# Two FFN pairs' last products put in a row on TensorE, in a hybrid decoder layer on one Trainium2 core

## The chip, the cores and the metric

The kernel runs on one core of one Trainium2 chip. The metric is the device time of one execution in microseconds, as the median over runs. Engines are named as in the profile: PE is TensorE's matmul, PEld its weight load, DVE is VectorE, ACT ScalarE, POOL GpSimd, SP SyncE, which here issues nearly all DMAs.

## What is computed

One layer of a decoder trunk: a token mixer (mLSTM beside attention over a memory), then a squared-ReLU MLP, each behind an RMSNorm and with a residual sum, and a last RMSNorm. The change lies in the first matrix product of the MLP.

```
D_MODEL = 1024; SEQ = 1024; D_FF = 4 * D_MODEL          # all float32
def squared_relu_mlp(h, w1, w2):
    return jnp.square(jax.nn.relu(h @ w1)) @ w2
x = x + mlstm_mixer(rms_norm(x, norm_mix0), mem_k, mem_v, ...)
x = x + squared_relu_mlp(rms_norm(x, norm_ffn0), w_ff1_0, w_ff2_0)
return rms_norm(x, final_norm)
```

## The kernel before

**Number format.** Every float32 operand of a matmul is split into a high and a low part of the type fp32r: the high part is a copy by ScalarE (L88, L91, L806), the low part the difference between source and high part (L103, L771, L809), on VectorE or GpSimd. `mm3` (L108) then makes three matmuls, high times high (L110), high times low (L111), and low times high (L112). So the first matmul of a product waits for the left operand's high part, the third for its low part.

**The MLP's first product.** The hidden features come in 16 pairs of two 128-row blocks, the tokens in two halves of 512. Each pair is a 2 x 2 block product, computed with seven products instead of eight (the Strassen-Winograd scheme). Products have the names "1" to "7". Product i is `product1` (L871): four blocks of the contraction by `mm3`, twelve matmuls of 128 x 512 into one PSUM bank. Their left operands come from the weights: 1, 2 and 4 are the blocks 11, 12 and 22 themselves; 5, 6, 7 and 3 are the sums S1, S2, S3 and S4. `w_parts` (L694) loads the raw blocks, makes the sums (L722), and `make` (L751) splits them. The sums lie in three buffers (tag "sum"), the raw blocks in rings of their own, the split operands in five buffers (tag "w"). The right operands (B11, B21, B22, T1 to T4) are made once from the two halves of the normed input; T3 and T4 lie in the tile xa, and the parts of T4 and B22 are made last, by `other_half` (L799), which is a generator: `go_on(n)` (L1022) takes n of its steps.

**One pair's result.** Bank X collects products 1, 6, 7 and 4 one after the other, and is copied out in between; Y holds product 2, and Z 5 and 3. The sums are

- `first_part` (L938), `second_part` (L962), `third_part` (L969), `product5` (L977), `product7` (L981): products 1, 2, 6, 5, 7 with the copies out of X
- `sixth_part` (L985): h22 = copy + Z (L991), squared ReLU, writes of the planes 0 and 6
- `fourth_part` (L998): product 4, h21 by squared ReLU out of X, write of plane 1
- `fifth_part` (L1004): product 3, h12 = copy + Z (L1007), squared ReLU (L879, L880), four sums for the second matrix product (L1011 to L1014), and one write of four planes, 1 MB (L1015)

A pair's results go into a tile hq of seven planes (tag "qk", two buffers in all), and from there to HBM (hd). Pairs 0 to 5 have had products 1 and 2 beforehand, in `early` (L885), while the second half's input was normed. In all texts here 4_0 means product 4 of pair 0.

**The order.** The loop over ROW (L1026) runs the pairs 0, 1, 6, 2, 7, 3, ... and writes the products out by hand, pair by pair; matmuls of `product1` and some VectorE operations keep that order (`tc.keep_in_program_order`). All others are placed by a scheduler, which takes the code's order as its starting point and each engine's list is then run strictly in order. On TensorE the products around the change stand as 6_0, 5_0, 7_0, 6_1, 5_1, 7_1, 4_0, 1_6, 3_0, 4_1, 2_6, 3_1, 6_6, 5_6, 7_6, 6_2, 4_6. For pair 0 and pair 1 the low parts are VectorE's (`lows`, `on`). `first_part_of` (L84) puts each high part behind the one before it on ScalarE, through `queue`.

Of the kernel before, what the change touches and what calls it, by code (L numbers as in the profile page):

```python
# [8 lines left out]
F32 = mybir.dt.float32  # L9
F32R = mybir.dt.float32r  # L10
AF = mybir.ActivationFunctionType
# [3 lines left out]
P = 128  # L15
# [3 lines left out]
HT = 512  # L19
# [16 lines left out]
def trunk_kernel(ctx, tc, a, out):  # L36
    nc = tc.nc
    V, A, G, T = nc.vector, nc.scalar, nc.gpsimd, nc.tensor
# [3 lines left out]
    qkx = ctx.enter_context(tc.tile_pool(name="qkx", bufs=2))  # L42
# [4 lines left out]
    def ps(name):  # L47
        return psum.tile([P, 512], F32, tag="ps", name=name)
# [33 lines left out]
    queue = []  # L82
# [609 lines left out]
    ROW = [0, 1, 6, 2, 7, 3, 8, 4, 9, 5, *range(10, NPAIR)]  # L692

    def w_parts(pool, srcs, nm, homes=None, on=None, both=None, on_v="36"):  # L694
# [51 lines left out]
            for key in keys:  # L746
                load(key)

        get.again = again

        def make(i, lows):  # L751
            if i == "1":
# [125 lines left out]
    def relu_square(dst, src):  # L878
        A.activation(dst, src, AF.Relu)  # L879
        A.activation(dst, dst, AF.Square)  # L880
# [57 lines left out]
    def first_part(p):  # L938
        o = begun.get(p) or Pair()
        o.w = pair_parts(p, on=V if p == 1 else None) if p else a0  # L940
        if p not in begun:
            o.p, o.X, o.Y, o.Z = p, ps(f"fX{p}"), None, None
            product1(o.X, o.w("1"), "1", True)
        if p == 0:
            o.s = [None, hraw[0][:, 1], hraw[1][:, 0]]
        elif p == 1:
            o.s = [None, hraw[1][:, 1], cm.tile([P, HT], F32, tag="rms_r", name="hs_1")]
        elif p == ROW[2]:
            o.s = [hraw[0][:, 0], None, None]
        else:  # L950
            home(o)
        if p in begun:
            o.s[0] = o.s0
        else:
            A.activation(o.s[0], o.X, AF.Copy)
        return o

    def home(o):
        o.h = qkx.tile([P, 7, HT], F32, tag="qk", name=f"hq{o.p}")
        o.s = [o.h[:, SLOT[i]] for i in "173"]  # L960

    def second_part(o):  # L962
# [14 lines left out]
    def product5(o):  # L977
        o.Z = ps(f"fZ{o.p}")
        product1(o.Z, o.w("5"), "5", True)

    def product7(o):  # L981
        product1(o.X, o.w("7"), "7", False)
        A.activation(o.s[2], o.X, AF.Copy)  # L983

    def sixth_part(o):  # L985
        if o.p < 2:
            o.h = qkx.tile([P, 7, HT], F32, tag="qk", name=f"hq{o.p}")
        else:
            product7(o)
        h22 = o.h[:, SLOT["3"]]  # L990
        V.tensor_tensor(h22, o.s[2], o.Z, ALU.add)  # L991
        if o.p in begun:
            relu_square(o.h[:, SLOT["1"]], o.s[0])
        relu_square(h22, h22)
        for n in (0, 6):
            nc.sync.dma_start(hd[o.p, :, n], o.h[:, n])

    def fourth_part(o):  # L998
        product1(o.X, o.w("4"), "4", False)
        h21 = o.h[:, SLOT["2"]]  # L1000
        relu_square(h21, o.X)
        nc.sync.dma_start(hd[o.p, :, 1], o.h[:, 1])

    def fifth_part(o):  # L1004
        product1(o.Z, o.w("3"), "3", False)
        h12 = o.h[:, SLOT["7"]]
        st["h12"] = V.tensor_tensor(h12, o.s[1], o.Z, ALU.add).ins  # L1007
        relu_square(h12, h12)
        if o.p < NPAIR - 2:
            h11, h21, t2, t1, _, t4, h22 = (o.h[:, n] for n in range(7))  # L1010
            V.tensor_tensor(t1, h12, h11, ALU.subtract)  # L1011
            V.tensor_tensor(h12, h22, h12, ALU.subtract)
            V.tensor_tensor(t2, h22, t1, ALU.subtract)
            V.tensor_tensor(t4, h21, t2, ALU.subtract)  # L1014
            nc.sync.dma_start(hd[o.p, :, 2:6], o.h[:, 2:6])  # L1015
        else:
            nc.sync.dma_start(hd[o.p, :, 4], o.h[:, 4])

    begun, steps, sum_up = early()
    begun, old = {o.p: o for o in begun}, None  # L1020

    def go_on(n):  # L1022
        for _ in range(n):
            next(steps, None)

    for p in ROW:  # L1026
        cur = first_part(p)
        if p == 0:
            cur.w.again("12", "22")
            third_part(cur)  # L1030
            sum_up(begun[BEGUN - 1])
            go_on(4)
            product5(cur)
            go_on(2)
            product7(cur)
        elif p == 1:
            third_part(cur)
            go_on(1)
            product5(cur)
            go_on(3)  # L1040
            product7(cur)
            go_on(4)
            sixth_part(old)
            fourth_part(old)
            first = old
        elif p in begun:
            third_part(cur)
            fourth_part(old)
            fifth_part(old)
            product5(cur)  # L1050
            sixth_part(cur)
        else:
            if p == ROW[2]:
                go_on(4)
                sixth_part(old)
                fifth_part(first)
            fourth_part(old)
            second_part(cur)
            fifth_part(old)
            third_part(cur)  # L1060
            product5(cur)
            sixth_part(cur)
        old = cur
# [69 lines left out]
    last_pair, old = old, None  # L1133
    queue.clear()
    for c in range(NCH - 1):
        rights = {}
        for q in range(2):
# [3 lines left out]
            cur = quarter_first(c, q, rights)  # L1141
# [19 lines left out]
            old = cur  # L1161
# [134 lines left out]
```

## Time and profile before

| | us |
|---|---|
| runs: lowest, median, highest of 3 | 1080.66, 1084.4, 1086.15 |
| the profiled execution | 1080.86 |
| its span, first to last instruction | 1079.1 |
| busy in the span: PE, PEld | 1041.6, 888.9 |
| busy in the span: DVE, POOL, ACT | 704.8, 601.2, 547.4 |

The mean granted TensorE clock is 0.985 of full speed. Times in the rows count from the span's start. In a timeline a row is one instruction, or several alike ones merged (x2); its columns are start, duration, engine, line, operation, output and inputs, and in brackets how long the engine was idle before it and who released it. Buffer numbers are left out, so that w_a is any left operand of the MLP's first product and S_a any sum.

### The profile page before, as it was taken

Reading aid. Unit: us, or ns where it says so; the run is one execution under the profiler, and the core shown is the slowest. Engines: PE = TensorE matmul, PEld = TensorE weight load, DVE = VectorE, ACT = ScalarE, POOL = GpSimd, SP = SyncE. Lnnn points to the kernel's source line nnn. Section 1 sums busy time; section 2 is a strip of 40 time slices with the busy share of each in tenths; the row PEclk is TensorE's granted clock in tenths of the full one; section 3 lists DMA queues with packets and bytes.
Section 4 is the critical chain, followed back from the end, with each engine's and each line's share of the span. In section 5 each row is a group of like instructions: output and inputs, shape, how many; then the busy total and the mean of one; then the engine's idle time right before and its main releaser. Section 6 shows DMA issues by size and latency. Waiting matters only on the chain.

```text
span 1079.1 us, 14619 instructions
## 1 busy us (share of the span) xinstructions
PE 1041.6 (97%) x5014; PEld 888.9 (82%) x5014; DVE 704.8 (65%) x1139; ACT 547.4 (51%) x1062; POOL 601.2 (56%) x457
## 2 busy tenths in 40 slices
PE   9989999999999999987999999999999999999995
PEld 7988898899998888865888888887878888888894
DVE  6586885952767467983544343443889888878567
ACT  6376664344754454563555555555355334443273
POOL 6546434554434474012755656555678777786446
PEclk9998999999999999998999999999999999999997
DMA  7444342233323566214654544346756555544224
GB/s 214 106 132 132 91 127 80 67 99 89 91 67 107 161 192 195 78 58 162 200 181 170 195 166 157 127 156 233 252 189 196 152 160 163 150 136 136 60 70 155
DMA packets 81802, 152.46 MB, mean 141 GB/s; under 512 B 8096, under 2 KB 27584, under 8 KB 79936
## 3 DMA queue, kind: packets, MB, share of 16 engines
q1 hardware_dynamic: 81584, 151.51, 44.7%
q8 instruction: 39, 0.64, 0.2%
q14 instruction: 35, 0.29, 0.1%
q10 hardware_dynamic: 144, 0.03, 0.0%
HBM read 114.52 MB, written 36.19 MB: 140 GB/s over the span
## 4 chain that ended last, share of the span: by engine, by line
PE 77%; DVE 9%; DMA 6%; ACT 3%; issue 2%; POOL 2%; SPq 0%; DVEq 0%; POOLq 0%; ACTq 0%
PE fX L112 5%; PE fX L110 5%; PE fX L111 5%; PE gX L110 4%; PE gX L111 4%; PE gX L112 4%; DMA hr<-hd 4%; PE wo L110 3%; PE wo L112 3%; PE wo L111 3%; PE fZ L110 2%; PE fZ L112 2%; PE fZ L111 2%; PE gZ L111 2%; PE gZ L112 2%
## 5 line engine op out<-in xcount | busy, mean ns | idle before, releaser
L116 DVE TENSOR_TENSOR hb<-hr,hb 128x1024 fp32r<-128x1024 f32 x53 | 87.6, 1653 | 10.6 <-ACT hb L115 10.3
L1094 DVE TENSOR_TENSOR xo<-xo,gX 128x512 f32<-128x512 f32 x112 | 74.5, 682 | 26.1 <-PE gX L112 22.8
L111 PE MATMUL gX<-hb,w_b 128*128 128x512 f32 x224 | 87.3, 390 | 0.5 <-DVE hb L116 0.5
L110 PE MATMUL gX<-hb,w_b 128*128 128x512 f32 x224 | 86.2, 391 | 0.6 <-DVE xo L1094 0.6
L112 PE MATMUL gX<-hb,w_b 128*128 128x512 f32 x224 | 85.2, 390 | 0.8 <-POOL w_b L771 0.8
L91 ACT ACTIVATE w_b<-S_b 128x512 fp32r<-128x512 f32 x56 | 34.8, 629 | 75.9 <-PE gX L112 31.8
L771 POOL TENSOR_TENSOR w_b<-r_b,w_b 128x512 fp32r<-128x512 f32 x42 | 68.2, 1636 | 8.6 <-ACT w_b L91 8.6
L103 POOL TENSOR_TENSOR w_wo<-r_wo,w_wo 128x512 fp32r<-128x512 f32 x32 | 45.3, 1423 | 49.1 <-ACT w_wo L91 47.7
L115 ACT ACTIVATE hb<-hr 128x1024 fp32r<-128x1024 f32 x53 | 55.8, 1053 | 33.1 <-DMA hr<-hd 32.8
L771 POOL TENSOR_TENSOR w_a<-r_a,w_a 128x512 fp32r<-128x512 f32 x30 | 39.8, 1327 | 52.8 <-ACT w_a L88 52.0
L722 POOL TENSOR_TENSOR S_b<-r_b,r_b 128x512 f32<-128x512 f32 x28 | 46.5, 1661 | 28.8 <-DVE w_b L771 24.7
L103 POOL TENSOR_TENSOR w_o<-r_o,w_o 128x384 fp32r<-128x384 f32 x32 | 34.4, 1081 | 47.1 <-ACT w_o L91 47.1
L112 PE MATMUL fX<-xa,w_a 128*128 128x512 f32 x128 | 51.7, 404 | 7.7 <-DVE w_a L771 7.7
L103 POOL TENSOR_TENSOR w_v<-r_v,w_v 128x388 fp32r<-128x388 f32 x32 | 40.0, 1261 | 33.4 <-ACT w_v L91 33.3
L103 POOL TENSOR_TENSOR w_qk<-r_qk,w_qk 128x384 fp32r<-128x384 f32 x32 | 38.5, 1219 | 25.9 <-ACT w_qk L91 25.8
L88 ACT ACTIVATE w_a<-S_a 128x512 fp32r<-128x512 f32 x63 | 39.1, 625 | 24.8 <-PE fZ L112 14.5
L110 PE MATMUL fX<-xa,w_a 128*128 128x512 f32 x128 | 51.1, 399 | 0.2 <-ACT hq L983 0.2
L111 PE MATMUL fX<-xa,w_a 128*128 128x512 f32 x128 | 51.2, 400 | 0.0
L110 PE MATMUL wo<-xa,w_wo 128*128 128x512 f32 x128 | 51.0, 399 | 0.0
L110 PEld LDWEIGHTS gX<-hb,w_b 128*128 128x128 f32 x224 | 42.1, 188 | 10.3 <-DVE xo L1094 1.7
L112 PEld LDWEIGHTS gX<-hb,w_b 128*128 128x128 f32 x224 | 42.0, 188 | 10.0 <-POOL w_b L771 1.2
L111 PE MATMUL wo<-xa,w_wo 128*128 128x512 f32 x128 | 50.1, 391 | 0.0
(392 smaller groups left out, 3471.6 us busy)
## 6 DMA issues: line engine op xcount, KB each, us to landing
hr<-hd SPq DMA_DIRECT2D x53, 512.0 KB, 3.7
hd<-hq SPq DMA_DIRECT2D x14, 1024.0 KB, 4.1
r_b<-w_ff SPq DMA_DIRECT2D x56, 256.0 KB, 2.9
hd<-hq SPq DMA_DIRECT2D x50, 256.0 KB, 2.0
r_a<-w_ff SPq DMA_DIRECT2D x36, 256.0 KB, 2.7
r_wo<-w_out SPq DMA_DIRECT2D x32, 256.0 KB, 2.7
r_a<-w_ff SPq DMA_DIRECT2D x13, 512.0 KB, 4.5
r_v<-w_v SPq DMA_DIRECT2D x32, 194.0 KB, 2.4
```

What stands on the lines that cost most here:

```text
L88: i = A.activation(dst, src, AF.Copy)
L91: A.activation(dst, src, AF.Copy)
L103: i = engine.tensor_tensor(w[:, 1, :n], raw[:, :n], w[:, 0, :n], ALU.subtract)
L110: keep(T.matmul(out, lhsT=lh, rhs=rh, start=start, stop=False, skip_group_check=goes_on))
L111: keep(T.matmul(out, lhsT=lh, rhs=rl, start=False, stop=False, skip_group_check=goes_on))
L112: keep(T.matmul(out, lhsT=ll, rhs=rh, start=False, stop=stop, skip_group_check=goes_on))
L115: A.activation(hi, src, AF.Copy)
L116: V.tensor_tensor(lo, src, hi, ALU.subtract)
L722: i = (on or G).tensor_tensor(t, x, y, op)
L771: low = engine.tensor_tensor(w[:, 1], src, w[:, 0], ALU.subtract)
L1094: V.tensor_tensor(x, x, banks[e], ALU.add)
```

## The change

Nothing is added to or taken from the work; it is put in another order.

- `get.add_up` becomes callable from the loop, and `result(o)` allocates a pair's tile hq on its own.
- In pair 0's turn, pair 1's first part is begun before product 7 of pair 0: its sums S1 and S2 and the left operand of 6_1 are made there. ScalarE's copy of 7_0 out of the bank is placed behind that left operand's high part.
- In pair 1's turn, the left operand of 4_0 is made right behind the code of 5_1. 4_0 then comes before pair 0's sum h22, no longer behind it.
- At the head of pair 6's turn (ROW[2]) stand 4_1, the left operands of 3_0 and 3_1, then 3_0 with pair 0's last sums, and pair 1's h22. Only then comes pair 6's own first part.

On TensorE the products then stand as 6_1, 5_1, 7_1, 4_0, 4_1, 3_0, 1_6, 2_6, 3_1, 6_6, 5_6, 7_6, 6_2, 4_6. Lines behind L983 have other numbers in the new kernel: L991 becomes L994, L1007 L1010, L1011 to L1014 L1014 to L1017, L1015 L1018.

```diff
-        get.again = again
+        get.again, get.add_up = again, add_up
...
+    def result(o):
+        o.h = qkx.tile([P, 7, HT], F32, tag="qk", name=f"hq{o.p}")
+
     def home(o):
-        o.h = qkx.tile([P, 7, HT], F32, tag="qk", name=f"hq{o.p}")
+        result(o)
         o.s = [o.h[:, SLOT[i]] for i in "173"]
...
     def product7(o):
         product1(o.X, o.w("7"), "7", False)
-        A.activation(o.s[2], o.X, AF.Copy)
+
+        with tc.issue_after(queue[-1]) if o.p == 0 else nullcontext():
+            A.activation(o.s[2], o.X, AF.Copy)
 
     def sixth_part(o):
-        if o.p < 2:
-            o.h = qkx.tile([P, 7, HT], F32, tag="qk", name=f"hq{o.p}")
-        else:
+        if o.p >= 2:
             product7(o)
...
+    nxt = None
     for p in ROW:
-        cur = first_part(p)
+        if p == ROW[2]:
+
+            result(old)
+            old.w("4")
+            fourth_part(old)
+            go_on(4)
+            first.w("3")
+            old.w("3")
+            fifth_part(first)
+            sixth_part(old)
+        cur, nxt = nxt or first_part(p), None
         if p == 0:
             cur.w.again("12", "22")
             third_part(cur)
@@ -1032,16 +1046,21 @@
             go_on(4)
             product5(cur)
             go_on(2)
+            nxt = first_part(1)
+            nxt.w.add_up()
+            go_on(1)
+            nxt.w("6")
             product7(cur)
         elif p == 1:
             third_part(cur)
-            go_on(1)
             product5(cur)
+            old.w("4")
             go_on(3)
             product7(cur)
             go_on(4)
+            result(old)
+            fourth_part(old)
             sixth_part(old)
-            fourth_part(old)
             first = old
...
         else:
-            if p == ROW[2]:
-                go_on(4)
-                sixth_part(old)
-                fifth_part(first)
-            fourth_part(old)
+            if p != ROW[2]:
+                fourth_part(old)
             second_part(cur)
             fifth_part(old)
             third_part(cur)
```

**VectorE, from pair 0's h22 to 4_1's low part, before.** In the names w4_a0 is the left operand 4 of pair 0, S2_a1 the sum S2 of pair 1 (later S4 in the same place), hq0 pair 0's results, hs the copies out of the banks, B22 the last right operand, fZ0 bank Z of pair 0.

```order
L991 TENSOR_TENSOR hq0_4752<-hs_1_3952,fZ0_4645 128x512
L771 TENSOR_TENSOR w4_a0_4760<-r_a022_4623,w4_a0_4760 128x512
L809 TENSOR_TENSOR B22_0_3945<-x11_3991,B22_0_3945 128x512 x2
L809 TENSOR_TENSOR B22_1_3946<-x11_3991,B22_1_3946 128x512 x2
L991 TENSOR_TENSOR hq1_4807<-hs_1_4681,fZ1_4705 128x512
L771 TENSOR_TENSOR w3_a0_4816<-S2_a0_4166,w3_a0_4816 128x512
L1007 TENSOR_TENSOR hq0_4752<-hs_0_3951,fZ0_4645 128x512
L1011 TENSOR_TENSOR hq0_4752<-hq0_4752 128x512
L1012 TENSOR_TENSOR hq0_4752<-hq0_4752 128x512
L1013 TENSOR_TENSOR hq0_4752<-hq0_4752 128x512
L1014 TENSOR_TENSOR hq0_4752<-hq0_4752 128x512
L771 TENSOR_TENSOR w4_a1_4839<-r_a122_4679,w4_a1_4839 128x512
```

**The same place in the changed kernel**, as far as pair 0's h12.

```order
L994 TENSOR_TENSOR hq0_4755<-hs_1_3952,fZ0_4645 128x512
L771 TENSOR_TENSOR w4_a1_4779<-r_a122_4666,w4_a1_4779 128x512
L809 TENSOR_TENSOR B22_0_3945<-x11_3991,B22_0_3945 128x512 x2
L809 TENSOR_TENSOR B22_1_3946<-x11_3991,B22_1_3946 128x512 x2
L771 TENSOR_TENSOR w3_a0_4802<-S2_a0_4166,w3_a0_4802 128x512
L722 TENSOR_TENSOR S2_a1_4671<-r_a112_4662,S2_a1_4671 128x512
L994 TENSOR_TENSOR hq1_4778<-hs_1_4668,fZ1_4705 128x512
L771 TENSOR_TENSOR w3_a1_4806<-S2_a1_4671,w3_a1_4806 128x512
L1010 TENSOR_TENSOR hq0_4755<-hs_0_3951,fZ0_4645 128x512
```

The low part of 4_1 moved from behind pair 0's four last sums to a place ahead of the last right operand; those of 3_0 and 3_1 stand ahead of pair 0's h12 (L1010). The low part of 4_0 is no longer in this piece: it stands further up, beside 6_1's and 5_1's.

**VectorE behind that, in the changed kernel**, up to pair 0's last sum.

```order
L771 TENSOR_TENSOR w6_a6_4902<-S2_a6_4900,w6_a6_4902 128x512
L1014 TENSOR_TENSOR hq0_4755<-hq0_4755 128x512
L1015 TENSOR_TENSOR hq0_4755<-hq0_4755 128x512
L1016 TENSOR_TENSOR hq0_4755<-hq0_4755 128x512
L968 TENSOR_TENSOR hs_0_3951<-hs_0_3951,fY6_4861 128x512
L1017 TENSOR_TENSOR hq0_4755<-hq0_4755 128x512
```

Pair 0's last sum (L1017) stood right behind the three others and now stands behind the addition of 2_6 (L968), which reads fY6, its bank.

**GpSimd, pair 6's left operands, before** (w1_a6 belongs to 1_6, S1_a6 to S3_a6 are its sums, r_a its raw blocks).

```order
L771 TENSOR_TENSOR w1_a6_4787<-r_a611_4778,w1_a6_4787 128x512
L771 TENSOR_TENSOR w2_a6_4858<-r_a612_4780,w2_a6_4858 128x512
L722 TENSOR_TENSOR S1_a6_4898<-r_a621_4782,r_a622_4784 128x512
L722 TENSOR_TENSOR S2_a6_4900<-S1_a6_4898,r_a611_4778 128x512
L722 TENSOR_TENSOR S3_a6_4937<-r_a611_4778,r_a621_4782 128x512
L722 TENSOR_TENSOR S2_a6_4900<-r_a612_4780,S2_a6_4900 128x512
L771 TENSOR_TENSOR w5_a6_4922<-S1_a6_4898,w5_a6_4922 128x512
L771 TENSOR_TENSOR w7_a6_4939<-S3_a6_4937,w7_a6_4939 128x512
```

**The same in the changed kernel.**

```order
L722 TENSOR_TENSOR S1_a6_4898<-r_a621_4840,r_a622_4842 128x512
L722 TENSOR_TENSOR S2_a6_4900<-S1_a6_4898,r_a611_4836 128x512
L771 TENSOR_TENSOR w1_a6_4845<-r_a611_4836,w1_a6_4845 128x512
L722 TENSOR_TENSOR S3_a6_4937<-r_a611_4836,r_a621_4840 128x512
L771 TENSOR_TENSOR w2_a6_4862<-r_a612_4838,w2_a6_4862 128x512
L771 TENSOR_TENSOR w5_a6_4922<-S1_a6_4898,w5_a6_4922 128x512
L722 TENSOR_TENSOR S2_a6_4900<-r_a612_4838,S2_a6_4900 128x512
L771 TENSOR_TENSOR w7_a6_4939<-S3_a6_4937,w7_a6_4939 128x512
```

The low parts of 1_6 and 2_6 stood ahead of the sums of pair 6 and stand between them now.

## Rows read from the trace of the kernel before

**Rows 1.** The page, part 1: busy us (share) xinstructions, by engine.

```profile
PE 1041.6 (97%) x5014; PEld 888.9 (82%) x5014; DVE 704.8 (65%) x1139; ACT 547.4 (51%) x1062; POOL 601.2 (56%) x457
```

**Rows 2.** Who TensorE waited for, 460 to 516 us: us in total, times, longest.

```profile
PE fX L112 <- DVE w_a L771: 7.7, 2, 5.0
PE fZ L110 <- ACT w_a L88: 2.0, 1, 2.0
PE fX L110 <- ACT w_a L88: 1.2, 1, 1.2
```

**Rows 3.** Windows: us; busy (x) of PE, PEld, DVE, ACT, POOL; clock, DMA, GB/s.

```profile
479.20:482.90 3.70, 3.70 (x10) 2.46 (x8) 3.60 (x6) 0.63 (x1) 0.96 (x1) 0.54 0.63 213
...
494.80:499.90 5.10, 4.92 (x12) 3.86 (x13) 0.12 (x1) 0.26 (x1) 0.00 (x0) 0.50 0.74 257
499.90:507.70 7.80, 5.76 (x24) 4.16 (x23) 2.58 (x4) 4.40 (x8) 2.34 (x2) 1.00 0.41 114
507.70:516.00 8.30, 8.30 (x38) 6.87 (x37) 6.64 (x7) 3.63 (x8) 6.96 (x6) 1.00 0.61 212
```

**Rows 4.** Timeline of PE: 7_0's last matmul, the first of six products.

```profile
465.46 0.39 PE L112 MATMUL fX<-xa,w_a 128*128 128x512 f32 x1
...
470.18 0.39 PE L110 MATMUL fZ<-T,w_a 128*128 128x512 f32 x1
...
472.90 0.39 PE L110 MATMUL fX<-xa,w_a 128*128 128x512 f32 x1
...
475.62 0.39 PE L110 MATMUL fX<-xa,w_a 128*128 128x512 f32 x1
...
489.32 0.39 PE L110 MATMUL fX<-xa,w_a 128*128 128x512 f32 x1
...
507.73 0.39 PE L110 MATMUL fX<-T,w_a 128*128 128x512 f32 x1
...
515.89 0.39 PE L110 MATMUL fX<-T,w_a 128*128 128x512 f32 x1
```

**Rows 5.** Timeline of DVE, 463 to 515 us.

```profile
464.69 0.69 DVE L722 TENSOR_TENSOR S_a<-S_a,r_a 128x512 f32<-128x512 f32 x1
...
476.59 0.69 DVE L991 TENSOR_TENSOR hq<-hs,fZ 128x512 f32<-128x512 f32 x1
477.20 1.64 DVE L771 TENSOR_TENSOR w_a<-r_a,w_a 128x512 fp32r<-128x512 f32 x1
...
489.52 0.69 DVE L1007 TENSOR_TENSOR hq<-hs,fZ 128x512 f32<-128x512 f32 x1 [5.77 <-PE fZ L112]
491.57 0.69 DVE L1011 TENSOR_TENSOR hq<-hq 128x512 f32<-128x512 f32 x1 [1.36 <-ACT hq L880]
...
494.23 0.69 DVE L771 TENSOR_TENSOR w_a<-r_a,w_a 128x512 fp32r<-128x512 f32 x1
...
512.97 1.78 DVE L1013 TENSOR_TENSOR hq<-hq 128x512 f32<-128x512 f32 x1
```

**Rows 6.** Timeline of POOL.

```profile
477.02 1.27 POOL L771 TENSOR_TENSOR w_a<-r_a,w_a 128x512 fp32r<-128x512 f32 x1 [2.47 <-ACT w_a L88]
...
512.58 1.63 POOL L722 TENSOR_TENSOR S_a<-S_a,r_a 128x512 f32<-128x512 f32 x1
```

**Rows 7.** Timeline of ACT: copy of 7_0, high parts of 6_1 and 5_1.

```profile
465.89 0.60 ACT L983 ACTIVATE hs<-fX 128x512 f32<-128x512 f32 x1 [2.56 <-PE fX L112]
466.38 1.14 ACT L88 ACTIVATE w_a<-S_a 128x512 fp32r<-128x512 f32 x2
```

**Rows 8.** DMA: KB, median us to landing; hd's landings; pair 2's load.

```profile
hd<-hq SPq DMA_DIRECT2D x6, 1024.0 KB, 4.2
...
r_a<-w_ff SPq DMA_DIRECT2D x6, 512.0 KB, 5.0
...
DMA to landing us min/median/max: 2.0/2.2/6.1
...
504.68 0.38 SPq L708 DMA_DIRECT2D r_a<-w_ff  x1
```

## Prediction before the run

> **What bounds the kernel now.** I began with the page's busy times: TensorE has work in 97% of the span [rows 1], so an edit gains only where TensorE waits. Then I read TensorE's waits for the stretch from the end of pair 0's product 7 to pair 2's product 6 [rows 2]. I write 4_0 for product 4 of pair 0. The two longest, 7.7 us together (5.0 and 2.7), are for the second (low) part of a left operand made on VectorE; waits of 2.0 and 1.2 for ScalarE's high parts follow. Third comes the granted clock by stretch [rows 3]: 0.54 for 3.7 us after the wait of 2.7, 0.50 for 5.1 us after that of 5.0 (half of full speed, 1.2 of 2.4 GHz), and 1.00 in the stretch with the wait of 2.0. Fourth comes TensorE's timeline [rows 4], for the total. 5_1 starts at 470.18 and 7_1 at 472.90, so a product at full clock takes 2.72 us, twelve matmuls of 0.227. Pair 0's product 7 ends at 465.46 + 0.23 = 465.69; 6_6 starts at 507.73. Between lie nine products, 24.5 us of work in 42.04 us: **17.56 us are lost**, and that is all the change can win here. By parts: 465.69 to 475.62 (three products) loses 1.77; to 489.32 (4_0, 1_6, 3_0) 5.54; to 507.73 (4_1, 2_6, 3_1) 10.25. Slow clock is in it: twelve matmuls in 5.10 us [rows 3] is 0.2 us more for each.
>
> Why the waits are there, VectorE's timeline shows [rows 5]. The low part of 4_0 starts at 477.20, behind the sum h22 of pair 0 (476.59), and takes 1.64 us because a GpSimd operation runs from 477.02 [rows 6]. The low part of 4_1 starts only at 494.23, behind five operations of pair 0's last sums (489.52 to 494.23), which need 3_0 to be finished. It needs none of them: VectorE works in order.
>
> **The change, part by part.** No instruction is added or taken away; all is order.
>
> *6_1.* ScalarE's copy of pair 0's product 7 started at 465.89 and 6_1's high part behind it at 466.38 [rows 7]. Now the high part stands ahead. The sum it needs was done at 465.4 [rows 5], so it runs 0.6 us or more earlier, and a little of the wait for the low part stays. Of the 1.77 us lost, 1.06 stay (bounds 0.4 and 1.77).
>
> *4_0, 4_1, 3_0 in a row.* Their low parts now stand on VectorE ahead of every sum that needs one of these products. Replaying VectorE's new order with 0.60 us for one operation after another and the old releases, 4_0's low part is done near 469, 4_1's at 477.7 and 3_0's at 480.7. TensorE wants them at 475.4, 478.1 and 480.9 (469.5 for 5_1, then 2.72 a product, third matmul 0.45 in). Margins of 0.4 and 0.2 us are thin, but a slip costs only its own size. I take 0. The half clock goes with the waits that preceded it. So 1_6 starts at 483.1.
>
> *1_6 and 2_6.* Their low parts are made on GpSimd, and its new order puts the sums of pair 6 among them. S2 of pair 6 takes the buffer that 3_0's low part reads last, free at 480.7. S2 to about 482.5, 1_6's low part from 483.0 to 484.3, S3 to 486.7, 2_6's low part to 488.5: operations of 1.27 us [rows 6], with a VectorE operation between each two. TensorE wants the low parts at 483.5 and 487.1, so it waits **0.8 and 1.5 us** (bounds 0.3 to 1.8 and 0.3 to 2.5: a VectorE operation less or more before each).
>
> *7_6.* It must wait until ScalarE has copied 6_6 out of the bank into hq6, and hq6 takes the buffer of hq0 (two buffers). That is free when hq0's last write, 1 MB, has landed: 4.2 us [rows 8]. The write waits for the last of pair 0's sums, which now stands behind the addition of 2_6. With GpSimd beside it, VectorE's sums take 1.8 us each instead of 0.7: 512.97 against 491.57 [rows 5], GpSimd's own taking 1.63 [rows 6]. So: 3_0 done 483.1, h12 added 485, relu and square 487.2, three sums to 493, addition of 2_6 493.9, last sum 494.5 and issue at 495.2, landed 499.4, relu and copy 500.6. TensorE has finished 5_6 at 498.9: **1.7 us**, in a place where it did not wait before. Bounds: 0 if VectorE runs unhindered; 1.7 + 2.0 if the write takes the slowest landing of these writes, 6.1 [rows 8].
>
> Here a rule speaks against the change. The Trainium skill, SBUF — State Buffer, "Who interferes with whom", says that a VectorE operation with two SBUF inputs and a GpSimd operation that reads SBUF shut each other out for a whole instruction. The trace agrees (1.78 us beside GpSimd, 0.69 us alone). Without that rule the three sums and all behind them would be through some 3 us earlier, 7_6 would not wait, and 2_6 would wait about 0.9 less: the sum below would be -13.3 us.
>
> *6_2.* The load of pair 2 stands behind hq0's write on the DMA queue: issued about 495.8, landed 5.0 us later [rows 8], two sums on GpSimd (2.6) and ScalarE's high part (0.6) give 504.0, against 503.3 on TensorE: 0.6, and 0.3 for the low part (bounds 0 to 2.1). The following pairs run some 11 us earlier with their loads moved up less; for small waits there I put 0.9 (0 to 2).
>
> **Sum.** Removed 17.56 - 1.06 = 16.5; new 0.8 + 1.5 + 1.7 + 0.9 + 0.9 = 5.8; net **-10.7 us**. Behind it TensorE is full [last row of rows 3], so nothing waits there to swallow it, and nothing off TensorE ends the kernel. The profiled execution took 1080.86 us (1079.1 span, 1.8 around it): 1070.2. It is 3.5 below the median of the runs shown, 1084.4, which spread over 5.5 us. Between 1070.2 and 1084.4 - 10.7 = 1073.7 I take 1071.5.
>
> **Rivals.**
> A. *The new waits are long enough to halve the clock.* The gaps of 0.8, 1.5 and 1.7 us lie within 18 us. For it: the wait of 2.7 us was followed by 0.54 [rows 2, 3]. Against: the wait of 2.0 us was followed by 1.00. Price: new waits at their upper ends, 1.8 + 2.5 + 3.7 + 2.1 + 2 = 12.1, and one spell of 3.4 us at half clock (eight matmuls, 1.6): 13.7 new, -2.8 net, so 1078; with waits half way there, 1075. The Trainium skill, TensorE: Matmul & The Clock Gate, "A second HAM failure mode", says that short idles between groups of matmuls, if frequent enough, make the clock swing; by that rule this rival is the case, and the rows here bear it out only for a wait over 2 us.
> B. *GpSimd is not in the way*, because its operations fall between VectorE's: 7_6 does not wait, 2_6 little, later pairs not at all: -14 us, 1067. Against: GpSimd has eight operations for pair 6 in the 12 us in which VectorE has pair 0's chain.
> C. *Slower: loads become the bound of the whole row.* Pair 2's load was issued at 504.68 [rows 8], 11.2 us before 6_2 at 515.89 [rows 4]; now 8.1 us before. Landing, two sums and high part take 8.2. If each of the 13 pairs behind pair 6 kept so short a lead and lost 1.3 us, that would be 17 us: 1087. It decides at a lead under about 7 us kept pair after pair. Against: only pair 2's load stands behind hq0's write, and GpSimd and the DMA queue have slack to regain.
> D. *The change does not do what it says*: the scheduler keeps the old order. The listings above show the low parts moved; only their releases could undo it: no change, 1084.
>
> **How the numbers follow.** A measurement of this kernel tells about 0.5% from no change, 5.4 us, so faster means under 1079. Forecast 0.61, A 0.21, B 0.11, C 0.04, D 0.03. The range runs from the best sum (-14.5 on 1080.86, 1066.4, less a microsecond) to A's worst end and a little of the spread of the runs: 1065.5 to 1079. Outside lie C, D and tails, under 2 in 10. Faster: forecast, B and most of A, 0.89; within 0.5%: D and the rest of A, 0.07; slower: C, 0.04.
>
> **What would show it.** In the changed profile TensorE should have no wait for VectorE's low part in 4_0, 4_1 and 3_0, and no half clock between 475 and 505. Right if the low part of 1_6 and of 2_6 waits for GpSimd (about 1 us each), and ScalarE's first write into hq6 waits for a DMA of hd, with TensorE waiting for the copy of 6_6. VectorE's sums of pair 0 should show 1.6 to 1.8 us where GpSimd is busy. 6_2 should start near 504. Wrong if a wait over 2.5 us appears with a clock of 0.5, if waits for loads recur pair after pair (C), or if the stretch is clean and the time still does not fall.

## Result and profile after

The changed kernel takes **1068.64 us** (median of six runs, 1068.23 to 1070.04). The kernel before, with three more runs on the same chip, takes 1080.06 (six runs, 1078.81 to 1086.15). The ratio is 0.9878 with an interval of 0.9861 to 0.9895: 1.2% faster (by the medians 11.4 us, 1.1%); no change, 1.0, lies outside that interval. Forecast were 1071.5 us, 1065.5 to 1079.0.

The profiled execution of the changed kernel took 1068.74 us, with a span of 1067.0 and a mean granted clock of 0.988. The span is 12.1 us shorter than before. The page's busy times [rows 1] hardly moved:

```profile
PE 1039.1 (97%) x5014; PEld 887.6 (83%) x5014; DVE 702.7 (66%) x1139; ACT 546.5 (51%) x1062; POOL 601.0 (56%) x457
```

TensorE's waits in the changed kernel from 440 us to the end (in all, times, longest), to be held against [rows 2]. Names with g are banks of the MLP's second product, w_b and hb its left and right operands, xo its running sums:

```profile
PE gX L112 <- POOL w_b L771: 1.9, 1, 1.9
PE fX L110 <- ACT hq L978: 1.6, 1, 1.6
...
PE fX L110 <- ACT w_a L88: 0.8, 2, 0.5
```

The waits for VectorE's low parts, 7.7 us before, are gone, and so are the 2.0 in front of 3_1. New is 1.6 us for ScalarE's copy L978 (6_6 out of its bank, in front of 7_6); the 1.9 us for GpSimd lie in the MLP's second product, outside the changed stretch. TensorE's timeline, answering to [rows 4], has the first matmuls of 6_1, 4_0, 1_6, 2_6, 3_1, 7_6, 6_2 and 4_6:

```profile
465.73 0.50 PE L110 MATMUL fX<-T,w_a 128*128 128x512 f32 x1 [0.32 <-ACT w_a L88]
...
474.32 0.39 PE L110 MATMUL fX<-xa,w_a 128*128 128x512 f32 x1
...
482.48 0.39 PE L110 MATMUL fX<-B,w_a 128*128 128x512 f32 x1
...
485.43 0.39 PE L110 MATMUL fY<-B,w_a 128*128 128x512 f32 x1
...
488.41 0.39 PE L110 MATMUL fZ<-B,w_a 128*128 128x512 f32 x1
...
498.32 0.50 PE L110 MATMUL fX<-xa,w_a 128*128 128x512 f32 x1 [1.59 <-ACT hq L978]
...
501.84 0.50 PE L110 MATMUL fX<-T,w_a 128*128 128x512 f32 x1 [0.51 <-ACT w_a L88]
...
504.97 0.39 PE L110 MATMUL fX<-xa,w_a 128*128 128x512 f32 x1
```

From 474.32 to 482.48 are 8.16 us, three products of 2.72 with nothing between them: 4_0, 4_1 and 3_0 run in a row without a loss. 1_6 takes 2.95 and 2_6 2.98, 0.23 and 0.26 over 2.72. 5_6 ends near 496.6 and 7_6 starts at 498.32: 1.75 lost. 6_2 starts 3.52 after 7_6, 0.80 over 2.72, and itself takes 0.41 over. From 465.25 to 501.84 the granted clock is 1.00; over the same microseconds of the kernel before it was 0.86.

I measure the changed stretch from the end of 7_0 to the start of 6_2: twelve products, 32.6 us of work. Before it took 515.89 - 465.69 = 50.20 us, now 501.84 - 465.25 = **36.59**, so 13.6 us are won there and 3.95 are still lost. 7_0 also ended 0.44 earlier, which I don't count for the change: in the changed kernel and runs 4 to 6, whose code is the same up to there, it ends between 465.23 and 466.08 (over all runs below between 463.8 and 466.1). Together 6_2 starts 14.05 us earlier, yet the span fell by 12.1. Of the 1.95 us between, 0.4 go in 6_2 itself; 4_6 starts 13.67 earlier, and that holds to the end of the MLP's first product. **1.5 us come back** in the second one: 0.2 in small pieces up to 785 us, where its work runs 13.46 earlier, and 1.3 from there to its last sums of squares, which run 12.13 earlier. The change doesn't touch that code. There two engines begin at the same moment, VectorE (L116) and GpSimd (L771). The timeline of both, before and in the changed kernel:

```profile
798.57 1.26 POOL L771 TENSOR_TENSOR w_b<-r_b,w_b 128x512 fp32r<-128x512 f32 x1
798.59 2.33 DVE L116 TENSOR_TENSOR hb<-hr,hb 128x1024 fp32r<-128x1024 f32 x1
```

```profile
785.09 1.21 DVE L116 TENSOR_TENSOR hb<-hr,hb 128x1024 fp32r<-128x1024 f32 x1
785.09 2.34 POOL L771 TENSOR_TENSOR w_b<-r_b,w_b 128x512 fp32r<-128x512 f32 x1
```

Before, GpSimd's operation took 1.26 us and VectorE's stretched to 2.33; now VectorE's took 1.21 and GpSimd's stretched to 2.34. TensorE waits there for GpSimd: 1.85 instead of 0.79 us. Behind the longer wait the granted clock is half for most of 4 us, which it wasn't before. The window in the changed kernel (columns as in [rows 3]), and under it the same place in a second profile of the same kernel (experiment 5):

```profile
787.48:791.40 3.92, 3.92 (x11) 3.11 (x12) 2.61 (x5) 2.85 (x4) 3.00 (x2) 0.61 0.78 206
```

```profile
790.02:794.00 3.98, 3.98 (x17) 3.30 (x18) 2.44 (x4) 2.42 (x3) 3.01 (x2) 1.00 0.77 205
```

Eleven matmuls instead of 17 in 3.9 us: six times 0.227 are 1.4 us. The first matmul of the product into gY behind it starts at 794.21 against 805.56 before, 11.35 earlier: 2.1 us are lost by then, the longer wait and the half clock less a wait of 0.26 us for xo that only the kernel before has. Behind that the kernel before waits for xo again (0.32 us) and starts more slowly after it, which gives 0.8 back, and 1.3 remain.

### The profile page after: what moved, and what is told of

It is laid out like the page before. It is cut to its first block, busy times and chain, and to the rows that moved or that the text cites. A ratio compares the mean times of both kernels' runs of the same rounds, so it can differ in the third digit from the quotient of the medians.

```text
span 1067.0 us, 14612 instructions
## 1 busy us (share of the span) xinstructions
PE 1039.1 (97%) x5014; PEld 887.6 (83%) x5014; DVE 702.7 (66%) x1139; ACT 546.5 (51%) x1062; POOL 601.0 (56%) x457
## 4 chain that ended last, share of the span: by engine, by line
PE 74%; DVE 10%; DMA 5%; ACT 4%; POOL 3%; issue 3%; SPq 0%; DVEq 0%; POOLq 0%; ACTq 0%
PE fX L112 5%; PE fX L110 5%; PE fX L111 5%; PE gX L112 4%; PE gX L110 4%; PE gX L111 4%; DMA hr<-hd 2%; PE wo L111 2%; PE wo L110 2%; PE wo L112 2%; PE fZ L112 2%; PE fZ L111 2%; PE fZ L110 2%; PE gZ L110 2%; PE gZ L111 2%
## 5 line engine op out<-in xcount | busy, mean ns | idle before, releaser
L116 DVE TENSOR_TENSOR hb<-hr,hb 128x1024 fp32r<-128x1024 f32 x53 | 86.1, 1625 | 12.3 <-ACT hb L115 12.1
L771 POOL TENSOR_TENSOR w_b<-r_b,w_b 128x512 fp32r<-128x512 f32 x42 | 69.5, 1666 | 7.9 <-ACT w_b L91 7.9
L115 ACT ACTIVATE hb<-hr 128x1024 fp32r<-128x1024 f32 x53 | 55.7, 1051 | 31.3 <-DMA hr<-hd 31.0
L722 POOL TENSOR_TENSOR S_b<-r_b,r_b 128x512 f32<-128x512 f32 x28 | 46.9, 1674 | 27.8 <-DVE w_b L771 24.2
L103 POOL TENSOR_TENSOR w_v<-r_v,w_v 128x388 fp32r<-128x388 f32 x32 | 38.7, 1222 | 32.8 <-ACT w_v L91 32.6
L771 POOL TENSOR_TENSOR w_a<-r_a,w_a 128x512 fp32r<-128x512 f32 x30 | 39.4, 1313 | 28.7 <-ACT w_a L88 27.9
L110 PE MATMUL fX<-xa,w_a 128*128 128x512 f32 x128 | 50.0, 391 | 1.8 <-ACT hq L978 1.6
L112 PEld LDWEIGHTS gX<-hb,w_b 128*128 128x128 f32 x224 | 42.3, 189 | 11.3 <-POOL w_b L771 2.3
L111 PEld LDWEIGHTS gX<-hb,w_b 128*128 128x128 f32 x224 | 42.4, 189 | 9.7 <-DVE hb L116 0.9
L771 POOL TENSOR_TENSOR w_b<-S_b,w_b 128x512 fp32r<-128x512 f32 x28 | 42.8, 1530 | 12.8 <-ACT w_b L91 12.8
L110 PEld LDWEIGHTS gX<-hb,w_b 128*128 128x128 f32 x224 | 42.6, 190 | 8.9
```

The costliest lines, as they stand in the source:

```text
L103: i = engine.tensor_tensor(w[:, 1, :n], raw[:, :n], w[:, 0, :n], ALU.subtract)
L110: keep(T.matmul(out, lhsT=lh, rhs=rh, start=start, stop=False, skip_group_check=goes_on))
L111: keep(T.matmul(out, lhsT=lh, rhs=rl, start=False, stop=False, skip_group_check=goes_on))
L112: keep(T.matmul(out, lhsT=ll, rhs=rh, start=False, stop=stop, skip_group_check=goes_on))
L115: A.activation(hi, src, AF.Copy)
L116: V.tensor_tensor(lo, src, hi, ALU.subtract)
```

## Experiments

Theory: TensorE lost its time because the low parts stood behind sums in VectorE's order; behind that, two limits are hidden, pair 0's 1 MB write (at 7_6) and pair 2's load (at 6_2). Rivals: the row of products itself is what counts; the write alone limits; GpSimd is not what slows VectorE's sums. Runs 1 to 4 shared one chip, 5 to 8 a second and 9 to 11 a third; each ratio is to the kernel before on that chip. "Stretch" is the time from the end of 7_0 to the start of 6_2, in the one profile of each run. The code of each run shows the lines that matter: dots stand for lines between, and one line may hold several of the kernel's.

**1. Pair 1 first, alone.** Kernel before with:

```diff
...
+            nxt = first_part(1); nxt.w.add_up(); go_on(1); nxt.w("6")
             product7(cur)
...
+        with tc.issue_after(queue[-1]) if o.p == 0 else nullcontext():
             A.activation(o.s[2], o.X, AF.Copy)
```

> The kernel before with one part of the change: ScalarE's high part of 6_1 ahead of its copy of 7_0. Theory (each place is a loss of its own, and the waits behind 6_1 are VectorE's order): the three products from the end of 7_0 to the start of 4_0 lose about 0.9 instead of 1.77 us, the waits of 5.0 and 2.7 us for VectorE's low parts stay within 0.5 us, and the time falls by 0.5 to 1 us (1079 to 1080). Rival (an earlier 6_1 moves everything behind it, and the long waits shrink by themselves): the two long waits fall by more than 2 us together, time under 1077.

1081.81 us, ratio 1.0 (0.9986 to 1.0013). Two of TensorE's waits:

```profile
PE fX L112 <- DVE w_a L771: 6.7, 2, 5.0
PE fX L110 <- ACT hq L879: 2.1, 1, 2.1
```

6_1 waits 0.31 instead of 1.20 and the wait of 5.0 stays, as expected. The time shows no fall: the medians differ by 0.3 us, and an interval of this width can't tell the 0.5 to 1 us that were expected. In this trace the first long wait is 1.65 instead of 2.7 and no half clock follows it, but 1_6 now waits 2.05 instead of 0.69 for ScalarE (L879). Neither theory gave that wait. The stretch is 2 us shorter in the one profile, and the runs don't show it. Open, for this order of the products.

**2. Operands early, products in the old order.** Run 1's kernel with:

```diff
             product5(cur)
+            old.w("4")
             go_on(3)
...
                 go_on(4)
+                first.w("3"); old.w("4"); old.w("3")
                 sixth_part(old)
                 fifth_part(first)
```

> As the run before, and the low parts of 4_0, 4_1, 3_0 and 3_1 made on VectorE ahead of the sums, but TensorE's products in their old order (4_0, 1_6, 3_0, 4_1, 2_6, 3_1). Theory (VectorE's order alone made the waits, the row of products adds little): no wait for VectorE over 0.7 us, and 1069 to 1072 us. Rival (the row matters, because it puts 1_6 and 2_6 later, when GpSimd has their low parts): TensorE waits over 2 us at 1_6 or 2_6, and 1073 to 1077 us.

1070.7 us, ratio 0.9896 (0.9873 to 0.9919); stretch 37.5 us. Nearly the whole gain is there without the row. No wait for VectorE is over 0.5 us. The longest wait left is 2.09 us, at 1_6; the rival named the place, not the cause and not the time. TensorE's row, then ScalarE's:

```profile
479.59 0.50 PE L110 MATMUL fX<-B,w_a 128*128 128x512 f32 x1 [2.09 <-ACT hq L879]
```

```profile
478.96 0.57 ACT L879 ACTIVATE hq<-fX 128x512 f32<-128x512 f32 x1
```

1_6 can't start until ScalarE has read 4_0 out of its bank (done 479.53): with eight banks in turn, pair 6's X is the one that pair 0 leaves, and the read stands behind four others on ScalarE. In the changed kernel 4_1 and 3_0 fill that time. This is what the row is worth, with the smaller wait at 7_6 here (0.69) set against it: 0.9 us of the stretch (37.5 against 36.6). The times can't tell so little: 0.9896 against 0.9878 and, in run 5, 0.9899. The kernel before had a wait of 0.69 us for L879 at the same place.

**3. The row, operands late.** Changed kernel with:

```diff
-            old.w("4")
             go_on(3)
...
             result(old)
-            fourth_part(old)
             sixth_part(old)
+            fourth_part(old)
...
-            result(old); old.w("4"); fourth_part(old); go_on(4)
-            first.w("3"); old.w("3"); fifth_part(first); sixth_part(old)
+            go_on(4); result(old); sixth_part(old); fourth_part(old); fifth_part(first)
```

> The changed kernel with the products in their new row, but the low parts of 4_0, 4_1, 3_0 and 3_1 made where the products are used, behind the sums. Theory (VectorE's order makes the waits): a wait of 1.5 to 2.7 us at 4_0 and one of 3 us or more at 4_1 for VectorE, some of it at half clock, so half of the gain or less: 1073 to 1077 us. Rival (the row of products is what counts): 1068 to 1070 us.

1076.28 us, ratio 0.9947 (0.9929 to 0.9966); stretch 43.3 us:

```profile
PE fX L112 <- DVE w_a L771: 3.6, 2, 2.2
PE fZ L110 <- ACT w_a L88: 2.1, 1, 2.1
```

The waits for VectorE are 1.46 at 4_0 and 2.16 at 4_1; the latter and the 2.11 at 3_1 are followed by a clock near 0.6. The second wait is shorter than expected, but half of the gain is gone with VectorE's order. Theory over rival.

**4. Short writes.** Changed kernel; pair 0's planes 2 to 5 are written one by one:

```diff
+            write = lambda n: nc.sync.dma_start(hd[o.p, :, n], o.h[:, n]) if o.p == 0 else None
             V.tensor_tensor(t1, h12, h11, ALU.subtract)
+            write(3)
             V.tensor_tensor(h12, h22, h12, ALU.subtract)
+            write(4)
             V.tensor_tensor(t2, h22, t1, ALU.subtract)
+            write(2)
             V.tensor_tensor(t4, h21, t2, ALU.subtract)
-            nc.sync.dma_start(hd[o.p, :, 2:6], o.h[:, 2:6])
+            write(5)
+            if o.p:
+                nc.sync.dma_start(hd[o.p, :, 2:6], o.h[:, 2:6])
```

> The changed kernel; only pair 0's last four results go out in four writes of 256 KB, each behind its sum, instead of one of 1 MB behind the last. Theory (7_6 waits because the buffer of hq0 is free only when the 1 MB has landed): the last piece lands 2 us sooner, TensorE's wait of 1.6 us for ScalarE's copy of 6_6 goes (under 0.3), and the time falls by 1.0 to 1.8 us against the changed kernel (1067 to 1067.6). Rival (the load of pair 2, queued behind, is next and as late): the wait at 6_2 grows from 0.5 to 1.5 us or more and the time stays within 0.5 us of 1068.6.

1068.66 us, ratio 0.9888 (0.9861 to 0.9915); stretch 37.4. The rival came:

```profile
498.98 0.50 PE L110 MATMUL fX<-xa,w_a 128*128 128x512 f32 x1 [0.91 <-ACT hq L978]
...
503.52 0.50 PE L110 MATMUL fX<-T,w_a 128*128 128x512 f32 x1 [1.52 <-ACT w_a L88]
```

```profile
503.52:508.20 4.68, 4.68 (x12) 3.41 (x13) 4.31 (x4) 2.62 (x5) 4.13 (x3) 0.64 0.59 187
```

7_6 waits 0.7 less, 6_2 1.0 more, and the clock fell to 0.64 behind it. Another 0.5 of this profile's longer stretch is a wait at 1_6 for GpSimd's low part (0.49), ahead of both places. So the write matters at 7_6, and 6_2 has a limit of its own.

**5. The changed kernel again**, no edit, on the chip of runs 6 to 8.

> The changed kernel once more, as the mark for the three runs beside it on this chip. Theory: 1068 to 1070 us, ratio to the kernel before 0.986 to 0.990, TensorE's waits from 6_1 to 6_2 as in its first profile (7_6 1.6, 6_2 0.5 us, each within 0.4). In the second FFN the wait for GpSimd's low part (1.9 us in the first profile, 0.8 in the kernel before) is a matter of which of VectorE and GpSimd starts first: between 0.3 and 2.0 us, and where it is over 1.5, GpSimd's operation there takes over 2 us and VectorE's beside it 1.2. Rival (the change itself makes that wait): 1.7 us or more again.

1069.87 us, ratio 0.9899 (0.9876 to 0.9922). The stretch repeats to 0.01 us (36.58; 7_6 1.58, 6_2 0.52). The GpSimd wait in the second product is 1.72, which fits both; runs 7 and 10 speak on it, and run 1, without most of the change, had 1.97.

**6. Copy aside.** Changed kernel with:

```diff
         if o.p == ROW[2]:
-            s0 = o.s[0]
+            s0, s1 = o.s[0], cm.tile([P, HT], F32, tag="acc", name="s1_6")
+            A.activation(s1, o.X, AF.Copy)
             home(o)
+            o.s[1] = s1
             relu_square(o.s[0], s0)
+            return
```

> The changed kernel, but ScalarE copies 6_6 out of its bank into a buffer of its own instead of hq6, so 7_6 no longer waits for pair 0's 1 MB write. Theory (two limits stand behind one another: that write, and pair 2's load that is issued only when 3_1 is finished): the wait at 7_6 goes from 1.6 to 0, the wait at 6_2 grows from 0.5 to about 2 us, 6_2 starts within 0.4 us of where it did (501.8, if 7_0 ends at 465.3), and the time is within 1 us of the changed kernel. Rival (the write alone holds it up): 6_2 starts 1.5 us earlier and the time falls by 1.3 to 1.8 us.

1071.6 us (1067.51 to 1072.44), ratio 0.9907 (0.9886 to 0.9927). ScalarE copies 6_6 at once, while the relu into hq6 still waits for the write (2.40 us). 7_6 doesn't wait, and 6_2 takes it all:

```profile
494.82 0.58 ACT L976 ACTIVATE s<-fX 128x512 f32<-128x512 f32 x1
497.81 0.63 ACT L879 ACTIVATE hq<-hs 128x512 f32<-128x512 f32 x1 [2.40 <-DMA hd<-hq]
```

```profile
502.46 0.50 PE L110 MATMUL fX<-T,w_a 128*128 128x512 f32 x1 [2.35 <-ACT w_a L88]
```

The stretch is 36.57 us, the changed kernel's to 0.02. Theory: the two limits end at the same place. The median is 1.7 us above the changed kernel's on this chip, where within 1 us was expected; the intervals overlap, and the stretch has no part in it.

**7. Copy aside and load early.** Run 6's kernel; 3_1 (with `parts[2] = pair_parts(2)` behind it) ahead of 2_6, pair 0's four sums as `last_sums`, and VectorE's order pinned:

```diff
-            second_part(cur)
-            fifth_part(old)
+            if p == ROW[2]:
+                fifth_part(old); parts[2] = pair_parts(2)
+                last_sums(first); second_part(cur); last_sums(old)
...
+        if o.p < 2:
+            tc.keep_in_program_order(i)      # pair 0's and 1's h12 and first sum
```

> As the run before, and the order turned so that pair 2's load comes early: 3_1 ahead of 2_6 on TensorE, pair 1's sum h12 ahead of pair 0's last sums on VectorE, pair 2's load ahead of pair 0's 1 MB write on the DMA queue. Theory (two limits, now both moved): no wait at 7_6, at 6_2 0.6 us or less, 6_2 starts about 34.3 us after the end of 7_0 instead of 36.6, and the time falls by 1.5 to 2.5 us against the changed kernel (1066 to 1067 us). Rival (the late write of hq0 now holds ScalarE's copy of 7_6 into hq6): a new wait of over 1.5 us at 4_6, and no gain.

**1066.6 us**, ratio 0.9867 (0.9844 to 0.9889), against 0.9899 for the changed kernel beside it. The queue's row and TensorE's (6_2):

```profile
488.00 0.38 SPq L708 DMA_DIRECT2D r_a<-w_ff  x1
```

```profile
497.96 0.39 PE L110 MATMUL fX<-T,w_a 128*128 128x512 f32 x1
```

Pair 2's load is issued 23.4 us after 6_1's start at 464.65 (in the changed kernel 27.2), 6_2 starts without a wait, and the stretch is 33.78 us, 2.8 less than in the changed kernel. No wait appears at 4_6, so the rival is out.

**8. Pair 6's sums and low parts on VectorE.** Changed kernel with:

```diff
-        o.w = pair_parts(p, on=V if p == 1 else None) if p else a0
+        o.w = pair_parts(p, on=V if p in (1, ROW[2]) else None) if p else a0
...
+        if p == ROW[2]:
+            cur.w.add_up(); cur.w("6"); cur.w("5")
```

> The changed kernel with pair 6's sums and low parts (GpSimd's eight operations of this stretch) on VectorE, so that GpSimd stands idle beside pair 0's last sums. Theory (a GpSimd operation beside it makes a VectorE sum of two SBUF operands slow): each of pair 0's four sums takes 0.6 to 0.75 us instead of 1.7 to 1.8. VectorE has some 6 us more to do in the stretch, so a wait for it is possible (2_6 or 7_6, up to 2 us): 1067 to 1071 us. Rival (the sums are slow because of the DMA traffic or TensorE's reads): they stay over 1.5 us.

1072.5 us, ratio 0.9924 (0.9901 to 0.9947), slower than expected. Pair 0's sums:

```profile
485.83 0.69 DVE L1014 TENSOR_TENSOR hq<-hq 128x512 f32<-128x512 f32 x1
...
487.04 0.69 DVE L1015 TENSOR_TENSOR hq<-hq 128x512 f32<-128x512 f32 x1
487.64 0.69 DVE L1016 TENSOR_TENSOR hq<-hq 128x512 f32<-128x512 f32 x1
```

They take 0.69 instead of 1.66 to 1.80. But no DMA ran in these 2.6 us either (share 0.00 from 485.83 to 488.43), so the rival needs another look, at two windows of the changed kernel: pair 0's first three sums, and pair 1's four (columns as in [rows 3], at the end clock, DMA share and GB/s):

```profile
485.94:491.10 5.16, 5.16 (x23) 4.24 (x23) 5.13 (x4) 0.97 (x2) 4.64 (x3) 1.00 0.53 183
494.29:497.04 2.75, 2.44 (x11) 1.69 (x9) 2.68 (x4) 0.00 (x0) 0.00 (x0) 1.00 0.95 269
```

With the DMA engines at 0.95 and GpSimd idle, four sums take 2.68 us; at 0.53 and with GpSimd busy for 4.64 us, three take 5.1. TensorE has matmuls for 5.16 of 5.16 us in the one and 2.44 of 2.75 in the other, nearly as much, so its reads hardly make the difference. GpSimd it is. The kernel is slower all the same (stretch 40.7 us), because ScalarE's high parts now wait for VectorE's list: TensorE waits 3.31 us at 7_6 for one.

**9. Load early alone.** Run 7's kernel without the copy aside.

> The changed kernel with the early load of pair 2 (3_1 ahead of 2_6, pair 1's h12 ahead of pair 0's last sums, the load ahead of the 1 MB write) but with ScalarE's copy of 6_6 back in hq6. Theory (two limits behind one another, and 7_6 waits for the landing of hq0's last write): the write is now issued 3 to 5 us later, so the wait at 7_6 grows from 1.6 to 3.5 us or more, partly followed by half clock, and hides the load: no wait at 6_2, 1069 to 1073 us, no faster than the changed kernel. Rival (each of the two steps is worth half of what both gave): no wait over 1.6 us, 1067.5 to 1068.5 us.

1072.61 us, ratio 0.9909 (0.9891 to 0.9926); stretch 39.1. The time is as expected, the cause only in part. TensorE's row and ScalarE's:

```profile
499.29 0.80 PE L110 MATMUL fX<-xa,w_a 128*128 128x512 f32 x1 [3.56 <-ACT hq L978]
```

```profile
496.05 0.63 ACT L88 ACTIVATE w_a<-S_a 128x512 fp32r<-128x512 f32 x1 [6.43 <-POOL S_a L722]
...
498.14 0.61 ACT L879 ACTIVATE hq<-hs 128x512 f32<-128x512 f32 x1
498.66 0.57 ACT L978 ACTIVATE hq<-fX 128x512 f32<-128x512 f32 x1
```

The scheduler put pair 2's high parts ahead of the copy on ScalarE, and these wait for GpSimd's sum of the load until 496.05. Pair 0's write is issued at 492.61, 28.1 us after the end of 7_0 instead of 27.1, so 1 us later and not 3 to 5, and lands 3.8 us later. In the changed kernel 7_6 starts 1.26 us behind the landing (497.06, 498.32); the same here would be 497.7, an estimate from these rows: about 2.1 us of the 3.7 lost at 7_6 are the write's, and 1.6 the order on ScalarE. So the load alone gains nothing in this order; in another it might have gained some.

**10. Both, again**, run 7's kernel beside run 9.

> Copy aside and load early together once more, beside the run with the load alone. Theory: no wait over 0.4 us from 6_1 to 6_2, 33.3 us between their first matmuls as before, 1065.5 to 1068 us, ratio to the kernel before 0.984 to 0.989. Rival (the first run of it was luck of the chip): 1069 to 1071 us, as the changed kernel.

**1065.52 us**, ratio 0.9852 (0.9835 to 0.9868); 33.27 us from 6_1 to 6_2, as in run 7 (33.31). This is the best version here; in run 7 it was 0.3% below the changed kernel on the same chip, and the 2.8 us of the stretch are 0.26%. Its GpSimd wait in the second product is 1.89 us where the same kernel had 1.14 in run 7: the kernel doesn't set that wait by itself. (The two ran on different chips.)

**11. Without pair 1's part.** Changed kernel with run 1's lines taken out.

> The changed kernel without its first part: 6_1's high part stands behind ScalarE's copy of 7_0 again, the rest as changed. Theory (each place is a loss of its own): 6_1 waits 1.2 us instead of 0.3, everything behind it comes 0.9 us later by the same waits (7_6 1.6, 6_2 0.5), 6_2 starts 37.4 to 37.6 us after the end of 7_0 instead of 36.6, and the time is 0.5 to 1.2 us above the changed kernel (about 1069.5 to 1070.5). Rival (the 0.9 us is swallowed at the next wait, as the limits at 7_6 and 6_2 hang on loads and writes issued earlier): 7_6's wait shrinks by 0.9 and the time is the changed kernel's.

1070.32 us, ratio 0.9894 (0.9878 to 0.991):

```profile
465.20 0.50 PE L110 MATMUL fX<-T,w_a 128*128 128x512 f32 x1 [1.20 <-ACT w_a L88]
...
501.51 0.50 PE L110 MATMUL fX<-T,w_a 128*128 128x512 f32 x1 [0.52 <-ACT w_a L88]
```

7_0 ends at 463.84, so the stretch is 37.67: 1.1 more than with this part, of which 0.9 is 6_1's wait. It is a loss of its own in the trace. The runs can't tell 1 us: 0.9894 lies between the 0.9878 and 0.9899 of the changed kernel.

## Why the prediction was right, by its steps

- **VectorE's order (4_0, 4_1, 3_0).** Forecast: no loss, thin margins of 0.4 and 0.2 us. Measured: 8.16 us for three products. Run 2 against run 3 shows that the operands' place does it. The rows of VectorE:

```profile
475.10 1.07 DVE L771 TENSOR_TENSOR w_a<-r_a,w_a 128x512 fp32r<-128x512 f32 x1
...
478.50 0.68 DVE L771 TENSOR_TENSOR w_a<-S_a,w_a 128x512 fp32r<-128x512 f32 x1
...
485.94 1.80 DVE L1014 TENSOR_TENSOR hq<-hq 128x512 f32<-128x512 f32 x1 [1.16 <-ACT hq L880]
487.77 1.66 DVE L1015 TENSOR_TENSOR hq<-hq 128x512 f32<-128x512 f32 x1
489.36 1.77 DVE L1016 TENSOR_TENSOR hq<-hq 128x512 f32<-128x512 f32 x1
...
491.65 0.68 DVE L1017 TENSOR_TENSOR hq<-hq 128x512 f32<-128x512 f32 x1
```

  The low part of 4_1 is done at 476.2 (forecast 477.7), that of 3_0 at 479.2 (480.7); with the third matmuls at 477.5 and 480.2 the margins were 1.3 and 1.0 us. The 2.0 us in front of 3_1 were counted as removed without a reason. They did go, because its sum S4 (L722) now starts at 479.10 on VectorE and no longer at 503.21, behind the addition of 2_6; in run 3, with the operands late, they are there again (2.11). What the row of products adds was not in the prediction's reasons: about 0.9 us through the bank that 4_0 leaves (run 2).
- **6_1.** Forecast: 1.06 us stay. Measured: 474.32 - 465.25 less 8.16 = 0.91.
- **1_6 and 2_6, the term that was mis-sized.** Forecast 0.8 + 1.5, measured 0.23 + 0.26. GpSimd's rows:

```profile
479.41 1.53 POOL L722 TENSOR_TENSOR S_a<-S_a,r_a 128x512 f32<-128x512 f32 x1 [3.79 <-ACT hq L879]
481.68 1.30 POOL L771 TENSOR_TENSOR w_a<-r_a,w_a 128x512 fp32r<-128x512 f32 x1 [0.74 <-ACT w_a L88]
482.92 1.31 POOL L722 TENSOR_TENSOR S_a<-r_a,r_a 128x512 f32<-128x512 f32 x1
484.19 1.75 POOL L771 TENSOR_TENSOR w_a<-r_a,w_a 128x512 fp32r<-128x512 f32 x1
...
488.85 1.74 POOL L771 TENSOR_TENSOR w_a<-S_a,w_a 128x512 fp32r<-128x512 f32 x1
```

  S2 started at 479.41, because its buffer was free 1.5 us sooner than the replay of VectorE's list gave. (VectorE's low part of 3_0, its last reader, ended at 479.18; the row names ScalarE's L879, which ended 0.06 later, at 479.24.) And the step "with a VectorE operation between each two" failed: S3 follows the low part of 1_6 without a gap, the low part of 2_6 follows S3, and it is done at 485.9 instead of 488.5. VectorE had little to put between: it waited for 3_0.
- **7_6.** Forecast 1.7 us by sums of 1.8 us and a 1 MB write; measured 1.75, with sums of 1.80, 1.66 and 1.77, the write issued at 492.36 and ScalarE let go by it at 497.15:

```profile
492.36 0.33 SPq L1018 DMA_DIRECT2D hd<-hq  x1
```

```profile
497.15 0.63 ACT L879 ACTIVATE hq<-hs 128x512 f32<-128x512 f32 x1 [2.89 <-DMA hd<-hq]
497.69 0.58 ACT L978 ACTIVATE hq<-fX 128x512 f32<-128x512 f32 x1
```

  From the last sum on everything came 2.2 to 2.8 us earlier than forecast, TensorE and the write alike, so the difference held. Some of that is luck: the write was issued 0.03 us behind the last sum instead of 0.7, and took 4.7 us to land instead of 4.2. What carried this term is that the sums are slow beside GpSimd, and run 8 shows it (0.69 with GpSimd idle). The rule of the Trainium skill that was weighed (SBUF — State Buffer, "Who interferes with whom"), by which such a sum and a GpSimd operation that reads SBUF contend, agrees with that.
- **6_2 and later pairs.** Forecast 0.6 + 0.3 at 6_2, with 6_2 starting near 504; measured 0.80 + 0.41, at 501.84. For the later pairs 0.9 was put and nothing came: 4_6 starts 13.67 us earlier than before (504.97 against 518.64), and the next wait of TensorE over 0.2 us, at 731.13 against 744.79, 13.66. "Behind it TensorE is full, so nothing waits there to swallow it" held for the first product, and failed for the second, which gave back 1.5 us in the profiled execution.
- **The sum.** Up to 6_2's start the forecast was -16.5 + 0.8 + 1.5 + 1.7 + 0.6 = -11.9, and the stretch gave -13.6: 1.8 more at 1_6 and 2_6, 0.15 at 6_1, 0.2 less at 6_2. Behind it, 1.2 were put (0.3 in 6_2, 0.9 for later pairs), and 0.4 came there and 1.5 in the second product. With 7_0's 0.44 that is the span's -12.1. The medians differ by 11.4, the forecast was 10.7: the gain in the stretch was put 1.7 too small, and what was not foreseen behind it took some of that back. That these two errors lie on opposite sides is luck. The forecast time lies 2.9 above the median: 0.7 by the gain, 0.8 because the median before is 1080.06 and not the profiled 1080.86, and 1.3 by the step towards the three runs' median of 1084.4. The range's lower end doesn't follow from its terms: with all of them at their lower bounds (0.4 at 6_1, 0.3 and 0.3 at 1_6 and 2_6, nothing else) the best sum is -16.6, not -14.5.

Of the rivals, **A** (half clock) did not happen where it was put, with waits of 1.6 us at most; it did at 787 us, outside the change. The reason given against it, a full clock behind 2.0 us, doesn't explain that: in run 4 a wait of 1.52 us at 6_2 was followed by 0.64. Why the 1.59 us at 7_6 were followed by 1.00 is not known. **B** (GpSimd not in the way) was half true: 1_6 and 2_6 hardly waited for it and the later pairs not at all, but VectorE's sums were slow beside it, and 7_6 paid. **C** (loads bound pair after pair) was right about the place, since pair 2's load is the limit behind the write (runs 6, 7), but it goes no further than 6_2. **D** did not happen.

## What to carry to other kernels

On an engine that works in order, look for what stands ahead of the operand that the full engine waits for, and move the operand, not the consumer: the left operands gave nearly the whole gain without the products being moved. When a wait is gone, ask for the next limit before mending the one that shows: freeing the write gained nothing alone, nor did hastening the load in the one order tried, and both together gained 2.8 us of the stretch. Look at the length of an edit's own stretch, which repeated to 0.03 us here, since waits elsewhere move by 2 us from one execution to the next; and look at the time as well, since a stretch 2 us shorter in one profile left it as it was (run 1).

## What was not expected of the hardware

- **The start of the second product varies by itself.** For one and the same kernel, TensorE's first wait there (for ScalarE's hb, L115) was none and 2.40 us (changed kernel, two profiles), or 0.17 and 2.37 (runs 7, 10). Its wait for GpSimd's low part 50 us later was 1.14 and 1.89 in runs 7 and 10, and 0.28 to 2.11 over all. In the eight profiles in which VectorE's L116 took 1.2 us beside it, it is 1.55 us or more; in the five others under 1.2. The Trainium skill (SBUF — State Buffer, "Who interferes with whom") says that issue order decides which of the two blocks. The rows at 798.57 and 798.59 agree: GpSimd started 0.02 us ahead and was not held up. At 785.09 both start alike to 0.01 us, so these rows show no order, and in run 6 the one that starts 0.01 later is not held up.
- **The length of one wait doesn't tell whether the clock falls.** Granted clock in the 3 to 5 us behind a wait, among others: 1.00 after 1.55, 1.72, 1.97, 2.0, 2.05 and 2.35 us (runs 2, 5, 1, before, 1, 6); 0.50 to 0.68 after 1.49, 1.52, 1.85, 1.89, 1.96, 2.11 and 2.16 us (runs 7, 4, changed kernel, 10, 8, 6, 3). The prediction had taken from [rows 2, 3] that only a wait over 2 us is followed by half clock; that does not hold. What TensorE had done before differs between most of these places. But at the second product's wait for GpSimd the same matmuls stand ahead, and there 1.72 and 1.97 us (runs 5, 1) were followed by 1.00, 1.85 and 1.96 (changed kernel, run 8) by 0.61 and 0.67. So the length alone doesn't decide; what does stays open.
